# Turning a norm's blocks by transfers between SBUF tiles, and scaling two tiles at once, in a two-layer encoder trunk

## The chip, the core and the metric

The kernel runs on one core of a Trainium2 chip. The metric is the device time of one execution in microseconds (us). Five engines work beside each other and wait for one another by semaphores: TensorE (PE) multiplies matrices, VectorE (DVE), ScalarE (ACT) and GpSimd (POOL) work on elements, and SyncE (SP) issues transfers. A tile lies in SBUF with 128 partitions; matrix products are collected in PSUM.

## The reference, cut to what matters

A trunk of two layers on x of 256 rows by 2048 features, in float32. Layer 0 mixes by attention, layer 1 by a recurrent block (RG-LRU); each is followed by a gated feed-forward block (FFN). Each mixer and each FFN begins with an RMS norm.

```python
def rms_norm(x, g):
    xf = x.astype(jnp.float32)
    y = xf * lax.rsqrt(jnp.mean(xf * xf, axis=-1, keepdims=True) + EPS)
    return (y * g.astype(jnp.float32)).astype(x.dtype)

def swiglu(h, w_gate, w_up, w_down):
    return (jax.nn.silu(h @ w_gate) * (h @ w_up)) @ w_down
...
    for i in range(DEPTH):
        h = rms_norm(x, norm_mix[i])
        ...
        x = x + mix
        x = x + swiglu(rms_norm(x, norm_ffn[i]), ffn_w_gate[i], ffn_w_up[i], ffn_w_down[i])
    return x
```

## The kernel before

**Precision.** Each factor of a product is held as two parts, hi (a cast) and lo (the rest), and three products of parts make one product. A weight arrives in pieces of 512 KB (`raw`, issued on SP); ACT casts it (`hi`, L145 or L163) and DVE subtracts (`lo`, L146 or L164). Pieces stand in a ring of a few buffers: a load leaves once its buffer is free, and a cast waits till PE has read an older piece. Some column pairs of the FFN are multiplied with seven products in place of eight; their weight sums are L169 to L171 and their sums of x are the forms below.

**Norms.** x lies with rows in the partitions (`x_tm`); the products need it with features in the partitions. So each of the three norms inside the program (FFN of layer 0, mixer of layer 1, FFN of layer 1) has four turns, one for each group g of 512 features, begun as soon as the residual of that group is added (L347 or L349). One turn:

- the squares of x with their sums, on ACT (L444);
- DVE transposes 32x32 blocks of the group into `one` (L408), one instruction of 128x1024;
- 16 copies of 32x256 elements bring each block to its place in `two` (L416). ACT and POOL take eight each, in the last turn of a norm DVE eight, ACT four and POOL four;
- `scale`: four tiles `xg`, each with the gain of its features multiplied in, hi on ACT (L435) and lo on DVE (L436);
- in the FFN norms, for six of eight pairs of tiles, `form`: ACT scales the pair again (L466), POOL makes four sums (L472), ACT and DVE split them into `fh` and `fl` (L474, L475).

The row factor of a norm (`nr`, L480 to L505) is applied behind the products. For the recurrent layer `spread` puts it on a diagonal (`dg`, L492, DVE) and PE broadcasts it (L493).

**Order.** PE's order is written by hand; the order on the other engines comes from a scheduler that follows the order of the code and estimated times. An engine executes its own order strictly, so a waiting instruction holds up all behind it, on SP too. `one` and `two` have one buffer each: a next turn waits till the last one is read. The units of the FFN use the same names for their sums (L769 to L795) and call the same `turn_blocks`, with copies on ACT; this call stays.

Of the kernel before, what the change touches and what calls it, by code (L numbers as in the profile page):

```python
# [12 lines left out]
F32 = mybir.dt.float32  # L13
F32R = mybir.dt.float32r
AF = mybir.ActivationFunctionType
ALU = mybir.AluOpType
AX = mybir.AxisListType

P = 128
S = 256  # L20
D = 2048
KT = D // P
# [11 lines left out]
WIDE = 512  # L34
# [4 lines left out]
NW = D // WIDE  # L39
# [35 lines left out]
def trunk(ctx, tc, w, out):  # L75
    nc = tc.nc
    act, dve, pool, pe, sync = nc.scalar, nc.vector, nc.gpsimd, nc.tensor, nc.sync
# [3 lines left out]
    xp = ctx.enter_context(tc.tile_pool(name="xp", bufs=16))  # L81
# [7 lines left out]
    def nm(s):  # L89
        uid[0] += 1  # L90
        return f"{s}_{uid[0]}"

    def tmp(tag, shape=(P, S), dt=F32, bufs=2):
        pl = tp if tag in COMMON else scope[-1]
        return pl.tile(list(shape), dt, tag=tag, name=nm(tag), bufs=bufs)


    newest = {}
# [25 lines left out]
    def behind(key, i):  # L124
        if key in newest:
            follow(i, newest[key])
        newest[key] = i
        for rule in [rule for rule in ahead if key == rule[2]]:
            rule[0] -= 1
            if rule[0] == 0:  # L130
                follow(i, rule[1])
                ahead.remove(rule)
# [251 lines left out]
    x_tm = cst.tile([P, 2, D], F32, tag="x", name="x")  # L384
# [15 lines left out]
    def col(name, i):  # L400
        o = PK[name] + i
        return pk[:, o : o + 1]


    def turn_blocks(src, engines, own=None, spread=None):
        turned = tmp("one", (P, 2, WIDE), bufs=1)
        own = tmp("two", (P, 2, WIDE), bufs=1) if own is None else own
        dve.transpose(turned, src)  # L408
        t = own.rearrange("p a (b c) -> p (a b) c", c=S)

        def move(i):
            of = turned[32 * i : 32 * i + 32].rearrange("p a (k j c) -> p k a j c", k=4, j=4)
            for j in range(4):
                to = t[32 * j : 32 * j + 32].rearrange("p k (a i c) -> p k a i c", a=2, i=4)
                eng = engines[(4 * i + j) % len(engines)]
                m = (eng.copy if eng is act else eng.tensor_copy)(to[:, :, :, i, :], of[:, :, :, j, :])  # L416
                if spread is not None:
                    behind("cast", m)

        for i in range(4):  # L420
            move(i) if spread is None else spread.append(partial(move, i))
        return t

    class Norm:
        def __init__(self, gname, gofs):
            self.g = (gname, gofs)
            self.xs = []
            self.ss = tmp("ssq", (P, 2, NW))
            self.forms = {}

        def scale(self, src):
            k = len(self.xs)
            g = col(self.g[0], self.g[1] + k)
            t = xp.tile([P, 2 * S], F32R, tag="xg", name=nm("xg"), bufs=16)
            newest["xh"] = act.activation(t[:, :S], src, AF.Copy, scale=g)  # L435
            newest["xl"] = dve.scalar_tensor_tensor(  # L436
                t[:, S:], src, g, t[:, :S].bitcast(F32), ALU.mult, ALU.subtract
            )
            self.xs.append(t)
# [6 lines left out]
        def add(self, g):  # L446
            for a in range(2):
                self.square(g, a)
            if g == NW - 1:
                self.finish()  # L450
            self.turn(g, (act, pool) if g < NW - 1 else (dve, act, dve, pool))
            if g == NW - 1 and self.g[0] == "norm_mix":
                held.extend([[4, "cast", newest["xh"]], [4, "rest", newest["xl"]]])

        def turn(self, g, engines):
            t = turn_blocks(x_tm[:, :, g * WIDE : (g + 1) * WIDE], engines)
            for k in range(4):
                self.scale(t[:, k, :])
            for i in range(2):
                if self.g[0] == "norm_ffn" and 2 * g + i in SEVEN:  # L460
                    self.form(2 * g + i, t[:, 2 * i : 2 * i + 2, :])

        def form(self, c, src):
            v, t = (tmp("form", (P, 2 * S)).rearrange("p (a b) -> p a b", a=n) for n in (2, 4))
            for j in range(2):
                act.activation(v[:, j, :], src[:, j, :], AF.Copy, scale=col(self.g[0], self.g[1] + 2 * c + j))  # L466
            (a11, a21), (a12, a22) = ([v[:, j, a * P : (a + 1) * P] for a in range(2)] for j in range(2))
            for i, x, y, op in (
                (0, a21, a22, ALU.subtract), (1, a11, a21, ALU.subtract),
                (2, t[:, 0, :], a11, ALU.subtract), (3, a12, t[:, 2, :], ALU.add),  # L470
            ):
                pool.tensor_tensor(t[:, i, :], x, y, op)  # L472
            hi, lo = (tmp(f"f{n}", (P, 4, P), F32R, bufs=len(SEVEN)) for n in "hl")
            act.copy(hi, t)  # L474
            dve.tensor_tensor(lo, t, hi[:].bitcast(F32), ALU.subtract)  # L475
            self.forms[c] = [(hi[:, i, :], lo[:, i, :]) for i in range(4)]
# [160 lines left out]
    def attend(h, acc, dst):  # L637
# [23 lines left out]
        def scores():  # L661
# [18 lines left out]
            def turn():  # L680
# [15 lines left out]
                later(d_val, values)  # L696

            later(d_turn, turn)

        later(d_split, partial(split, qs, q))  # L700
# [342 lines left out]
```

## Time and profile before

| | |
|---|---|
| median of 3 runs | 1953.04 us (1952.99 to 1953.76) |
| the profiled execution, its own time | 1952.89 us |
| its span | 1951.1 us, at full granted clock (1.00) |
| layer 0, turns of the FFN norm | residual adds from 219.63 to 268.14 us, transposes from 224.83 to 270.13 |
| layer 1, turns of the mixer's norm | residual adds from 911.26 to 951.59 us |
| layer 1, turns of the FFN norm | residual adds from 1216.62 to 1265.26 us |

The profile gives busy times of each engine, the chain of work that ended last, groups of equal instructions, what each engine waited for, the busy time of chosen stretches ("x112" is the number of instructions in it), and a timeline of single instructions, where the brackets at the end hold the idle time before an instruction and what ended it. Times run from the start of the span. PE started a matmul of 512 columns each 0.227 us where nothing held it up; that makes about 112 in 25 us.

### The profile page before, as it was taken

What the parts mean: (1) busy time and instruction counts of PE and PEld (TensorE: products, weight loads), DVE (VectorE), ACT (ScalarE), POOL (GpSimd) and SP (SyncE); (2) the same over time, 40 slices, a digit from 0 to 9 for tenths busy, and PEclk for the clock granted to TensorE, in tenths of its full rate; (3) what the DMA queues carried; (4) which work ended last, traced back from release to release, by engine and by line L of the source; (5) the groups of instructions that cost most, each with busy time, mean ns of one, the idle gap of its engine ahead of it and who ended that gap; (6) DMA issues with size and microseconds to landing.
All of it is one profiled execution on the core that took longest, in us unless ns stands there. A gap on an engine that the chain in (4) does not pass through costs nothing.

```text
span 1951.1 us, 27630 instructions
## 1 busy us (share of the span) xinstructions
PE 1938.0 (99%) x9224; PEld 1624.0 (83%) x9224; DVE 1768.6 (91%) x2417; ACT 1448.3 (74%) x2358; POOL 401.3 (21%) x497
## 2 busy tenths in 40 slices
PE   9999999999999999999999999999999999999999
PEld 8898888788888888888899998887888888888887
DVE  7878698999999999998799997898999999999993
ACT  7677686777777777777698887866778776787772
POOL 0442250011101111010465450520101111011100
PEclk9999999999999999999999999999999999999999
DMA  8434746698878978787365556555878888788872
GB/s 328 156 127 152 248 158 197 196 272 236 248 233 243 262 240 246 235 244 246 126 223 188 189 164 245 175 194 174 253 236 248 245 248 253 231 246 251 246 257 86
DMA packets 131727, 426.42 MB, mean 219 GB/s; under 512 B 14720, under 2 KB 14976, under 8 KB 131584
## 3 DMA queue, kind: packets, MB, share of 16 engines
q1 hardware_dynamic: 108944, 383.21, 58.0%
q0 software_dynamic: 22496, 41.43, 11.9%
q8 instruction: 72, 1.18, 0.2%
q14 instruction: 71, 0.58, 0.1%
q10 hardware_dynamic: 144, 0.02, 0.0%
HBM read 382.13 MB, written 2.10 MB: 197 GB/s over the span
## 4 chain that ended last, share of the span: by engine, by line
PE 92%; DVE 4%; ACT 1%; issue 1%; DMA 1%; POOL 0%; SPq 0%; ACTq 0%; DVEq 0%; POOLq 0%
PE acc L326 14%; PE acc L323 14%; PE acc L324 14%; PE pm L326 11%; PE pm L323 11%; PE pm L324 11%; PE acc L294 8%; PE acc L292 4%; PE pm L306 1%; PE pm L307 1%; PE pm L305 1%; DVE lo L146 1%; ACT hi L145 1%; DVE lo L164 0%; DMA raw<-in_w_in_dram 0%
## 5 line engine op out<-in xcount | busy, mean ns | idle before, releaser
L146 DVE TENSOR_TENSOR lo<-raw,hi 128x1024 fp32r<-128x1024 f32 (+1 forms) x474 | 574.5, 1240 | 77.1 <-ACT hi L145 75.3
L145 ACT CAST hi<-raw 128x1024 fp32r<-128x1024 f32 (+1 forms) x474 | 478.4, 1045 | 116.5 <-PE acc L324 72.1
L326 PE MATMUL acc<-lo,xg 128*128 128x512 f32 x744 | 290.9, 391 | 2.0 <-DVE lo L146 1.8
L323 PE MATMUL acc<-hi,xg 128*128 128x512 f32 x744 | 290.0, 390 | 0.0
L324 PE MATMUL acc<-hi,xg 128*128 128x512 f32 x744 | 289.6, 389 | 0.0
L164 DVE TENSOR_TENSOR lo<-raw,hi 128x1024 fp32r<-128x1024 f32 x232 | 275.0, 1217 | 6.5 <-ACT hi L163 3.8
L294 PE MATMUL acc<-xg,hi 128*128 128x512 f32 x832 | 271.7, 397 | 0.6 <-ACT hi L145 0.6
L163 ACT CAST hi<-raw 128x1024 fp32r<-128x1024 f32 x232 | 234.6, 1048 | 41.0 <-issue 14.4
L176 POOL DMA_DIRECT2D raw<-raw x90 | 77.7, 863 | 903.9 <-DVE raw L174 369.5
L323 PE MATMUL pm<-hi,act 128*128 128x512 f32 x512 | 199.2, 389 | 0.0
L324 PE MATMUL pm<-hi,act 128*128 128x512 f32 x512 | 199.2, 389 | 0.0
L326 PE MATMUL pm<-lo,act 128*128 128x512 f32 x512 | 199.2, 389 | 0.0
L416 ACT COPY two<-one 32x256 f32<-32x256 f32 x420 | 169.7, 404 | 24.7 <-DVE one L408 16.5
L292 PEld LDWEIGHTS acc<-xg,lo 128*128 128x128 f32 x832 | 156.3, 188 | 35.4 <-DVE lo L146 2.8
L323 PE MATMUL acc<-hi,act 128*128 128x512 f32 x448 | 174.9, 390 | 0.4 <-DVE two L794 0.4
L326 PE MATMUL acc<-lo,act 128*128 128x512 f32 x448 | 174.4, 389 | 0.0
L324 PE MATMUL acc<-hi,act 128*128 128x512 f32 x448 | 174.4, 389 | 0.0
L292 PE MATMUL acc<-xg,lo 128*128 128x256 f32 x832 | 171.8, 281 | 1.2 <-DVE lo L146 1.2
L326 PEld LDWEIGHTS acc<-lo,xg 128*128 128x128 f32 x744 | 139.7, 188 | 34.1 <-DVE lo L146 5.4
L324 PEld LDWEIGHTS acc<-hi,xg 128*128 128x128 f32 x744 | 139.7, 188 | 29.2
L323 PEld LDWEIGHTS acc<-hi,xg 128*128 128x128 f32 x744 | 139.7, 188 | 28.6
L170 ACT CAST hi<-raw 128x512 fp32r<-128x512 f32 x232 | 137.1, 622 | 32.8 <-DVE raw L169 31.8
(221 smaller groups left out, 3852.1 us busy)
## 6 DMA issues: line engine op xcount, KB each, us to landing
raw<-in_w_gate_dram SPq DMA_DIRECT2D x176, 512.0 KB, 4.6
raw<-in_w_up_dram SPq DMA_DIRECT2D x176, 512.0 KB, 5.5
raw<-in_w_down_dram SPq DMA_DIRECT2D x176, 512.0 KB, 4.4
raw<-in_w_in_dram SPq DMA_DIRECT2D x64, 512.0 KB, 4.4
raw<-raw POOLq DMA_DIRECT2D x90, 256.0 KB, 5.8
raw<-in_w_q_dram SPq DMA_DIRECT2D x32, 512.0 KB, 3.8
raw<-in_w_o_dram SPq DMA_DIRECT2D x32, 512.0 KB, 4.2
x<-form POOLq DMA_DIRECT2D x64, 256.0 KB, 6.7
```

What stands on the lines that cost most here:

```text
L145: behind("cast", act.copy(hi[:, sl], raw[:, sl]))
L146: behind("rest", dve.tensor_tensor(lo[:, sl], raw[:, sl], hi[:, sl].bitcast(F32), ALU.subtract))
L163: behind("cast", act.copy(hi, src))
L164: behind("rest", dve.tensor_tensor(lo, src, hi[:].bitcast(F32), ALU.subtract))
L170: behind("cast", act.copy(hi, o))
L176: pool.dma_start(out=t1, in_=b11, accum_op=ALU.add)
L292: pe.matmul(acc[:, S:], w, xs[k][:, :S], start=False, stop=stop)
L294: pe.matmul(acc, w, xs[k], start=(k == 0), stop=stop)
L323: pe.matmul(o, xh, wh, start=start, stop=False)
L324: pe.matmul(o, xl, wh, start=False, stop=False)
L326: pe.matmul(o, xh, wl, start=False, stop=stop)
L416: m = (eng.copy if eng is act else eng.tensor_copy)(to[:, :, :, i, :], of[:, :, :, j, :])
```

## The change

`turn` calls a new `move_blocks`. It transposes in two instructions, in an order in which the 1 KB that one block row takes lies in one run, so that each of the 16 blocks is moved as 32 runs of 1 KB. In eleven of the twelve turns SP issues these 16 moves as transfers from `one` to `two`; the last turn of the mixer's norm still copies on DVE, ACT and POOL. `scaled` treats two tiles at once: ACT writes the scaled pair (`form`, two instructions of 128x256), ACT casts it in one instruction of 128x512, DVE subtracts in another; `form` takes the scaled pair from there, so that the second scaling (L466) goes. The tiles `xg` come as eight pairs in place of sixteen.

```diff
+    def move_blocks(src, engines):
+        turned = tmp("one", (P, 2, WIDE), bufs=1)
+        own = tmp("two", (P, 2, WIDE), bufs=1)
+        one, two = (t.rearrange("p a b -> p (a b)") for t in (turned, own))
+        for a in range(2):
+            dve.transpose(
+                one.rearrange("p (j a e) -> p j a e", j=4, a=2)[:, :, a, :],
+                src[:, a, :].rearrange("p (k j c) -> p j k c", k=4, j=4),
+            )
+        for i in range(4):
+            for j in range(4):
+                to, of = two[32 * j : 32 * j + 32, S * i : S * i + S], one[32 * i : 32 * i + 32, S * j : S * j + S]
+                if engines is None:
+                    sync.dma_start(out=to, in_=of)
+                else:
+                    eng = engines[(4 * i + j) % len(engines)]
+                    (eng.copy if eng is act else eng.tensor_copy)(to, of)
+        return two.rearrange("p (i a k c) -> p k a i c", i=4, a=2, k=4)
...
+        def scaled(self, src):
+            k = len(self.xs)
+            v = tmp("form", (P, 2 * S)).rearrange("p (a b) -> p a b", a=2)
+            for j in range(2):
+                to = v[:, j, :] if len(src.shape) == 3 else v[:, j, :].rearrange("p (a i c) -> p a i c", a=2, i=4)
+                act.activation(to, src[:, j], AF.Copy, scale=col(self.g[0], self.g[1] + k + j))
+            t = xp.tile([P, 2, 2 * S], F32R, tag="xg", name=nm("xg"), bufs=KT // 2)
+            hi, lo = t[:, :, :S], t[:, :, S:]
+            newest["xh"] = act.copy(hi, v)
+            newest["xl"] = dve.tensor_tensor(lo, v, hi.bitcast(F32), ALU.subtract)
+            self.xs += [t[:, j, :] for j in range(2)]
+            return v
...
-            self.turn(g, (act, pool) if g < NW - 1 else (dve, act, dve, pool))
+            self.turn(g, (dve, act, dve, pool) if g == NW - 1 and self.g[0] == "norm_mix" else None)
...
-            t = turn_blocks(x_tm[:, :, g * WIDE : (g + 1) * WIDE], engines)
-            for k in range(4):
-                self.scale(t[:, k, :])
+            t = move_blocks(x_tm[:, :, g * WIDE : (g + 1) * WIDE], engines)
             for i in range(2):
+                v = self.scaled(t[:, 2 * i : 2 * i + 2])
                 if self.g[0] == "norm_ffn" and 2 * g + i in SEVEN:
-                    self.form(2 * g + i, t[:, 2 * i : 2 * i + 2, :])
-
-        def form(self, c, src):
-            v, t = (tmp("form", (P, 2 * S)).rearrange("p (a b) -> p a b", a=n) for n in (2, 4))
-            for j in range(2):
-                act.activation(v[:, j, :], src[:, j, :], AF.Copy, scale=col(self.g[0], self.g[1] + 2 * c + j))
+                    self.form(2 * g + i, v)
+
+        def form(self, c, v):
+            t = tmp("form", (P, 2 * S)).rearrange("p (a b) -> p a b", a=4)
```

In the new code the transposes are L429, the transfers L437, the copies that stay L440, the scaling L455, its cast L458 and its subtraction L459; lines behind the change are higher by 31 (L492 is L523, L480 is L511).

The order on SP in the changed kernel, where the second and third turns of layer 0's FFN norm are inserted among the loads of FFN weights (before, these loads followed each other without the two rows of L437):

```order
L140 DMA raw_3283<-in_w_gate_dram 128x1024
L437 DMA two_2744<-one_2743 32x256 x16
L140 DMA raw_3301<-in_w_up_dram 128x1024
L140 DMA raw_3319<-in_w_gate_dram 128x1024
L140 DMA raw_3337<-in_w_up_dram 128x1024
L140 DMA raw_3355<-in_w_gate_dram 128x1024
L437 DMA two_2937<-one_2936 32x256 x16
L140 DMA raw_3373<-in_w_up_dram 128x1024
```

Each block of 16 transfers stands whole between two loads, and the load behind it waits for the sixteen issues.

The order on ACT in the changed kernel at the last turn of the same norm, up to the first instruction of unit 0's end (L800, L769 before); L163 and L145 are weight casts, L505 is the cast `fh`, which waits for POOL's sums:

```order
L163 CAST hi_3447<-raw_3439 128x1024
L455 ACTIVATE form_3168<-two_3149,pk 128x256 x2
L458 CAST xg_3171<-form_3168 128x2x256
L170 CAST ohi_3451<-raw_3439 128x512
L505 CAST fh_3179<-form_3174 128x512
L455 ACTIVATE form_3183<-two_3149,pk 128x256 x2
L170 CAST hi_3453<-raw_3438 128x512 x2
L145 CAST hi_3486<-raw_3485 128x1024
L145 CAST hi_3509<-raw_3508 128x1024
L458 CAST xg_3186<-form_3183 128x2x256
```

Before, all four scalings of this turn stood ahead of the weight casts of its last two pairs; now the last pair's cast stands behind `fh` and two weight casts.

The order on DVE at the turn that keeps its copies, the last one of the mixer's norm, before:

```order
L436 SCALAR_TENSOR_TENSOR xg_9201<-two_9183,pk,xg_9201 128x256
L436 SCALAR_TENSOR_TENSOR xg_9204<-two_9183,pk,xg_9204 128x256
L436 SCALAR_TENSOR_TENSOR xg_9207<-two_9183,pk,xg_9207 128x256
L436 SCALAR_TENSOR_TENSOR xg_9210<-two_9183,pk,xg_9210 128x256
L349 SCALAR_TENSOR_TENSOR x<-acc_9214,nr_3161,x 128x512
L408 STREAM_TRANSPOSE one_9339<-x 128x1024
L480 TENSOR_REDUCE nm_9329<-ssq_3211 128x2
L416 COPY two_9340<-one_9339 32x8x32 x2
L485 TENSOR_SCALAR nm_9329<-nm_9329 128x2
L416 COPY two_9340<-one_9339 32x8x32 x6
```

and now, from the copies to `dg`:

```order
L440 COPY two_9321<-one_9320 32x256 x8
L459 TENSOR_TENSOR xg_9185<-form_9182,xg_9185 128x2x256
L459 TENSOR_TENSOR xg_9191<-form_9188,xg_9191 128x2x256
L511 TENSOR_REDUCE nm_9310<-ssq_3189 128x2
L516 TENSOR_SCALAR nm_9310<-nm_9310 128x2
L459 TENSOR_TENSOR xg_9343<-form_9340,xg_9343 128x2x256
L534 TENSOR_TENSOR rsq_s_9314<-nm_9310,nr_9313 128x2
L459 TENSOR_TENSOR xg_9349<-form_9346,xg_9349 128x2x256
L535 SCALAR_TENSOR_TENSOR rsq_s_9314<-rsq_s_9314,nr_9313 128x2
L536 SCALAR_TENSOR_TENSOR nr_9313<-rsq_s_9314,nr_9313 128x2
L146 TENSOR_TENSOR lo_9515<-raw_9513,hi_9514 128x1024
L523 TENSOR_SCALAR dg_9438<-ident,nr_9313 128x128 x2
```

The subtractions of the turn before (here L459 for `xg_9185` and `xg_9191`) stood ahead of the second add as four L436 and now follow the copies; the mean (L511) comes behind them, and one weight split stands ahead of `dg`.

More of the change, by code (lines that the diff above doesn't have):

```diff
@@ L433, in scale @@
             g = col(self.g[0], self.g[1] + k)
-            t = xp.tile([P, 2 * S], F32R, tag="xg", name=nm("xg"), bufs=16)
+            if k % 2 == 0:
+                self.pair = xp.tile([P, 2, 2 * S], F32R, tag="xg", name=nm("xg"), bufs=KT // 2)
+            t = self.pair[:, k % 2, :]
             newest["xh"] = act.activation(t[:, :S], src, AF.Copy, scale=g)
```

## The prediction

> **What bounds the kernel now.** I read the page's busy shares and chain first, then the stretches in which TensorE (PE) falls short, then what it waits for there.
>
> ```profile
> span 1951.1 us, 27630 instructions
> ...
> PE 1938.0 (99%) x9224; PEld 1624.0 (83%) x9224; DVE 1768.6 (91%) x2417; ACT 1448.3 (74%) x2358; POOL 401.3 (21%) x497
> ...
> PE 92%; DVE 4%; ACT 1%; issue 1%; DMA 1%; POOL 0%; SPq 0%; ACTq 0%; DVEq 0%; POOLq 0%
> ```
>
> PE is busy for 1938.0 of 1951.1 us, so about 13 us are all that any edit off PE can win; the diff leaves PE's instructions as they are. The chain agrees: 92% of it is PE. The question is where those 13 us lie, and whether the norms' turns are among them. Three stretches of 25 us, with the busy time of each engine:
>
> ```profile
> 275.00:300.00 25.00, 25.00 (x112) 20.71 (x111) 24.87 (x41) 17.95 (x34) 10.83 (x15) 1.00 0.51 152
> 350.00:375.00 25.00, 22.84 (x97) 17.61 (x96) 24.23 (x29) 15.56 (x24) 1.71 (x2) 1.00 0.65 193
> 950.00:975.00 25.00, 23.90 (x138) 20.41 (x137) 24.25 (x47) 15.12 (x28) 12.58 (x24) 1.00 0.47 161
> ```
>
> The last turn of layer 0's FFN norm falls into the first stretch: PE is busy for all of it. The second lies behind unit 0 of the FFN, without any norm turn, and loses 2.16 us. The third holds the turn ahead of the recurrent layer and loses 1.10 us. PE's longest sums of waits:
>
> ```profile
> PE pm L323 <- ACT ohi L170: 2.4, 2, 1.2
> PE acc L326 <- DVE lo L146: 1.8, 3, 0.8
> ```
>
> Both are waits for weight splits in the units, not for a norm. DVE's timeline in layer 1 shows that this lateness does not come from the turns:
>
> ```profile
> 1298.33 0.69 DVE L770 TENSOR_TENSOR one<-one,pm 128x512 f32<-128x512 f32 x1 [1.33 <-PE pm L326]
> ...
> 1305.06 0.69 DVE L794 TENSOR_TENSOR two<-acc,two 128x512 f32<-128x512 f32 x1 [0.29 <-PE acc L326]
> 1305.67 5.76 DVE L146 TENSOR_TENSOR lo<-raw,hi 128x1024 fp32r<-128x1024 f32 x5
> ```
>
> DVE twice stands idle for PE's banks after the turns are over, 1.33 and 0.29 us. Whatever lead a cheaper turn gives it ends there; it then falls behind through its own work (five splits in a row, 5.76 us), in an order that the change leaves alone.
>
> **The change, part by part.** Copies and scalings go, by these rows of what writes or reads `two` (min/median/max ns), with one price for a cast of 128x512:
>
> ```profile
> L416 ACT COPY two<-one x420: 395/404/409, 226.6 to 1896.4; 32x256 f32<-32x256 f32 x140
> L416 POOL COPY two<-one x84: 387/396/1302, 226.4 to 1271.9; 32x256 f32<-32x256 f32 x84
> L435 ACT ACTIVATE xg<-two,pk x48: 492/495/512, 234.7 to 1275.6; 128x256 fp32r<-128x256 f32 x48
> L436 DVE SCALAR_TENSOR_TENSOR xg<-two,pk,xg x48: 438/476/686, 236.0 to 1279.3; 128x256 fp32r<-128x256 f32 x48
> ...
> L416 DVE COPY two<-one x40: 280/286/533, 279.2 to 1897.8; 32x256 f32<-32x256 f32 x40
> L466 ACT ACTIVATE form<-two,pk x24: 493/497/511, 236.3 to 1281.6; 128x256 f32<-128x256 f32 x24
> L771 DVE TENSOR_TENSOR two<-one,pm x22: 679/680/689, 302.9 to 1876.2; 128x512 f32<-128x512 f32 x22
> ```
>
> ```profile
> L474 ACT CAST fh<-form 128x512 fp32r<-128x512 f32 x6 | 3.7, 614 | 2.8 <-POOL form L472 2.8
> ```
>
> The twelve turns held 84 copies on ACT, 84 on POOL and 24 on DVE; the last mixer turn keeps 4, 4 and 8. So ACT sheds 80 x 0.404 = 32 us, POOL 80 x 0.396 = 32 us, DVE 16 x 0.286 = 5 us. Scaling on ACT was 72 x 0.495 = 36 us (L435, L466) and becomes 48 such steps plus 24 casts, 24 + 24 x 0.614 = 39 us. On DVE 48 x 0.476 = 23 us become 24 x 0.680 = 16 us. Transposes stay at about the same elements. All of this relief is worth nothing to the end: it falls where PE is at x112 already, and stops at the two waits for PE above.
>
> What is added is 176 transfers on SP and their landing. Nearest prices from the DMA view (KB, us to landing):
>
> ```profile
> raw<-in_w_gate_dram SPq DMA_DIRECT2D x176, 512.0 KB, 4.6
> ...
> out_dram<-x SPq DMA_DIRECT2D x8, 256.0 KB, 2.0
> ```
>
> I bound a block copy of 32 KB by 2.0 and 4.6 us from its issue and take 2.5, near the smaller row, because its bytes are an eighth of that one's. SP's rows around the last two turns of layer 0, which are the places where a block is inserted:
>
> ```profile
> 262.71 0.33 SPq L140 DMA_DIRECT2D raw<-in_w_up_dram  x1
> ...
> 278.11 0.33 SPq L140 DMA_DIRECT2D raw<-in_w_up_dram  x1
> 290.32 0.33 SPq L140 DMA_DIRECT2D raw<-in_w_gate_dram  x1
> ```
>
> An issue takes 0.33 us; with the semaphore wait between two of them I take 0.4, so a block holds SP for 6.4 us and has landed 9 us after its first issue. The third turn's block goes ahead of the load of 262.71, which then leaves near 268.5, some 5.8 us late, and lands 4.6 us later at 273.1. Its cast is this row of ACT:
>
> ```profile
> 273.84 1.06 ACT L145 CAST hi<-raw 128x1024 fp32r<-128x1024 f32 x1 [1.20 <-PE acc L324]
> ```
>
> It waits for a place in the ring that PE frees, so the load is still on time, and PE is several halves behind. The fourth block goes between 278.11 and 290.32, into 12 us in which SP did nothing: it delays no load and lands near 287.4. PE first wants the sixth form and the last pair of tiles here:
>
> ```profile
> 299.03 0.39 PE L323 MATMUL pm<-hi,fh 128*128 128x512 f32 x1
> ...
> 302.43 0.39 PE L323 MATMUL acc<-hi,xg 128*128 128x512 f32 x1
> ```
>
> From 287.4 I count on ACT: two scalings and a cast, 1.6 us; POOL's four sums, 3.6 us; fh and fl, 1.3 us: the form is ready near 294, 5 us early. Behind it ACT does two scalings, two casts of 128x512 and two of 128x1024 before the last pair's cast, about 5 us: near 299, 3 us early. With the upper bound for each landing the eight transfers that may be on their way at once add 2.1 us to the ninth's issue and 2.1 to the end: 4.2 us later, so the form still comes by 298 and the last pair by about 303, half a microsecond late. Term: 0, at most 1 us a layer.
>
> **The turn that stays on the engines** is the one beside which PE has no cover. DVE and ACT before:
>
> ```profile
> 951.59 0.74 DVE L349 SCALAR_TENSOR_TENSOR x<-acc,nr,x 128x512 f32<-128x512 f32 x1
> 952.36 1.25 DVE L408 STREAM_TRANSPOSE one<-x 128x1024 f32<-128x1024 f32 x1
> ...
> 954.69 2.16 DVE L416 COPY two<-one 32x256 f32<-32x256 f32 x6
> ...
> 957.48 1.69 DVE L436 SCALAR_TENSOR_TENSOR xg<-two,pk,xg 128x256 fp32r<-128x256 f32 x4
> 959.20 0.48 DVE L492 TENSOR_SCALAR dg<-ident,nr 128x128 f32<-128x128 f32 x2
> ```
>
> ```profile
> 956.94 1.71 ACT L435 ACTIVATE xg<-two,pk 128x256 fp32r<-128x256 f32 x4 [1.13 <-DVE two L416]
> ```
>
> After, the second add no longer stands behind four L436 and starts about 1.6 us sooner, near 950.0; both transposes are done by 952.0, the eight copies (0.36 each) by 954.9. The earlier pairs' two subtractions now follow, to 956.1. ACT makes its four copies and two squares to 955.3, then, at 0.43 a scaling, four of these, two small steps of the root and two casts, to about 958.4. The second subtraction follows that cast, to 959.1, then two small steps and, new in this place, one weight split of 1.2 us ahead of L492. So dg starts near 960.5 to 960.8 where it started at 959.20: 1.3 to 1.6 later. PE there:
>
> ```profile
> 958.68 0.40 PE L294 MATMUL acc<-xg,hi 128*128 128x512 f32 x1
> 959.80 0.68 PE L493 MATMUL pm<-dg,ones 128*128 128x128 f32 x4 [0.73 <-DVE dg L492]
> ```
>
> ```profile
> 974.34 0.50 PE L292 MATMUL acc<-xg,lo 128*128 128x256 f32 x2 [0.37 <-DVE lo L146]
> ```
>
> L493 moves by the same 1.3 to 1.6. At 974.34 PE waits again, 0.37 us, for a split whose load left long before; a later PE waits there that much less. Net 0.9 to 1.2; bounds 0 (the contiguous copies run at DVE's smallest 0.28) and 2.5 (nothing absorbed, tiles late too).
>
> The Trainium skill has a rule on these copies ("VectorE: DVE Perf Modes", What auto-detection actually checks): one source and destination in SBUF with even outer dimensions already run two elements a cycle. By it the new shape gains nothing over the old one. No row of before has the new shape, so the trace cannot decide it. By the rule the sum below stays as it is; if the old shape was the slower one, it would be about 0.9 lower.
>
> **Sum:** 1952.89 (the profiled execution's own time) + 0 for the block transfers + 0.9 = 1953.8. That execution is 0.15 under the median of 1953.04, so no correction is made.
>
> **Rivals.** *Late blocks, slower.* If a small transfer's landing takes 7 us, the ninth issue of the fourth block waits until 285.9, the last leaves by 288.7 and lands at 295.7: 8.3 us later than I count, 3.3 to 5.3 more than the margins of 5 and 3. Two layers lose that much each, with the middle 1960 to 1964; it decides from about 5 us a landing. For it: the DMA row of 4.6 and the fact that weight loads fill the same queue just ahead. Against it: the margins, and loads whose readers wait for PE. Chance 0.16.
>
> The Trainium skill ("DMA: Bandwidth & Descriptors", Rules for kernel authors) says of many small transfers that under 64 KB one pays mostly overhead, and its section on queues that a completion signal lands behind earlier writes of the same DMA engine. Both speak for this rival; no transfer of this size between SBUF tiles is in the trace of before.
>
> *Relief reaches the units, faster.* If the lead on DVE and ACT outlives the waits at L770 and L794, the loss of the 350 stretch and its twin could halve: 2 x 2.16 / 2 = 2.2, with the splits behind them perhaps 4: 1949.8. Against it: the DVE rows of layer 1. Chance 0.10.
>
> *Nothing happens.* The copies are not what the end waits for, and the middle turn gains by its earlier transposes what it loses in order: 1952.9. Chance 0.20. My forecast, 1952.5 to 1955.5, has 0.48; the rest, 0.06, is a middle turn that costs over 2.5 us.
>
> **Numbers.** 0.2% is 3.9 us, about what a measurement of this kernel can tell from no change. Slower by more: 0.16 and a third of the last case, 0.18. Faster by more: some of the relief case, 0.06. Same: the rest, 0.76. The range goes from 1950.3, inside the relief case, to 1958.5, which leaves most of the late blocks out.
>
> **What would show it.** Right: x112 in the stretches from 225 to 300 as before; small transfers landing in 2 to 3 us; the wait of L493 for dg grown from 0.73 to about 2; the two unit stalls unchanged to a few hundredths. Wrong: PE waits for a norm's tiles or forms near 299 to 303, or at their like in layer 1; ACT idle for `two` by more than a few microseconds; load landings late ahead of L145; or less than 2 us lost at 350.

## The result and the profile after

The changed kernel took **1964.34 us** (median of 4 runs, 1963.08 to 1966.01) where the kernel before took 1953.01 us (4 runs, 1952.15 to 1953.76): a ratio of **1.0059, 95% interval 1.0041 to 1.0076**. It is slower, by 11.3 us, and lies 5.8 us above the upper end of the predicted range. The profiled execution took 1963.08 us, its span is 1961.3 us.

From the page after: span, busy shares, the chain by engine, and its shares by line.

```profile
span 1961.3 us, 27668 instructions
...
PE 1940.9 (99%) x9224; PEld 1624.8 (83%) x9224; DVE 1756.8 (90%) x2389; ACT 1420.6 (72%) x2278; POOL 354.2 (18%) x417
...
PE 87%; DVE 5%; ACT 3%; issue 2%; DMA 2%; SPq 1%; POOL 0%; ACTq 0%; DVEq 0%; POOLq 0%
PE acc L326 13%; PE acc L323 13%; PE acc L324 13%; PE pm L324 11%; PE pm L326 11%; PE pm L323 11%; PE acc L294 8%; PE acc L292 4%; DVE lo L146 2%; PE pm L306 1%; PE pm L307 1%; PE pm L305 1%; SPq L437 1%; ACT hi L145 1%; ACT two L416 1%
```

The relief came: DVE 11.8 us less and ACT 27.7, as the prediction's prices give (about 12 and 29), POOL 47.1 where they give 32. None of it shows in the time. Instead SP's queue, at 0% of the chain before, now holds 1% of it by the line of the new transfers (L437).

Where the 10.2 us of span went can be read by laying the two traces side by side: the same matmul, found by its place in PE's order (which the change leaves alone), starts so much later than before. At the times of the trace of before, in us:

| trace of before at | 200 | 290 | 304 | 320 | 346 | 900 | 957 | 960 | 975 | 1310 | 1365 | 1946 |
|---|---|---|---|---|---|---|---|---|---|---|---|---|
| after, later by | -0.27 | -0.27 | 1.84 | 2.31 | 2.89 | 2.79 | 9.62 | 10.47 | 10.03 | 10.15 | 10.43 | 10.23 |

Two places hold nearly all: **3.2 us between 290 and 346** (the end of layer 0's FFN norm) and **7.7 us around 957** (the norm ahead of the recurrent layer), of which 0.44 comes back at once. Layer 1's FFN norm costs 0.3. The same three stretches as before, with the busy time of PE, PEld, DVE, ACT and POOL, the granted clock, the DMA share and GB/s:

```profile
275.00:300.00 25.00, 24.24 (x107) 19.59 (x105) 19.39 (x29) 16.52 (x31) 9.80 (x13) 1.00 0.73 260
350.00:375.00 25.00, 22.81 (x97) 17.57 (x96) 24.20 (x30) 14.67 (x23) 1.22 (x2) 1.00 0.60 203
950.00:975.00 25.00, 18.86 (x94) 15.85 (x93) 16.72 (x32) 14.73 (x32) 5.44 (x13) 0.86 0.40 132
```

The first stretch was full (x112) and now is not (x107). The second, the stalls in the unit, is as it was (x97). The third has lost 44 matmuls, and its clock is at 0.86. What PE waited for (total, times, longest):

```profile
PE acc L294 <- DVE xg L459: 5.1, 1, 5.1
...
PE pm L324 <- DVE fl L506: 1.0, 1, 1.0
```

The largest wait is now a single one of 5.1 us for a norm's tile, and `fl` of a form is new in this list. Both are behind transfers. First the transfers themselves, from the view of line L437: min/median/max ns of one issue, and us from issue to landing.

```profile
L437 SPq DMA_DIRECT2D two<-one x176: 507/588/1772, 225.9 to 1294.8; - x176
...
DMA to landing us min/median/max: 1.7/1.9/8.2
```

The median landing is quick, 1.9 us, but 53 of the 176 took more than 2.5 us, one of them 8.2. The issue is slow everywhere: 0.588 us in the median, where the loads on which the prediction was built took 0.33. SP's queue, at the fourth block of layer 0, the three blocks ahead of the recurrent layer, and the fourth block of layer 1:

```profile
280.05 13.53 SPq L437 DMA_DIRECT2D two<-one  x16
...
917.90 11.21 SPq L437 DMA_DIRECT2D two<-one  x16
...
932.28 10.84 SPq L437 DMA_DIRECT2D two<-one  x16
...
946.24 10.29 SPq L437 DMA_DIRECT2D two<-one  x16
...
1283.04 12.31 SPq L437 DMA_DIRECT2D two<-one  x16
```

A block holds SP for 10 to 13.5 us; the prediction had 6.4. Where nothing else holds SP, one issue starts 0.63 us after the other, and 16 of them take 10.1. What the longer blocks have on top can be read from the start and the landing of each transfer. In all twelve traces of this case no more than eight transfers of SP and ACT together are under way at a time. Ahead of the fourth block of layer 0 stand nine loads of 512 KB that SP, held up by the third block, sent in 7 us (272.73 to 279.63); before, they left one by one from 262.71 to 278.11. They landed 4.4 to 9.1 us after their issue. The fourth to eighth transfers of the block start at 282.46, 283.74, 285.01, 286.29 and 288.01, each within 0.02 us of the landing of the load eight places ahead (282.45, 283.73, 285.00, 286.28, 287.99), and the first seven take 8.2 down to 3.5 us to land, against 1.9 for the last nine. So this block has 10.1 us of issues and 3.4 us of waits for loads to land; in the middle a block has 1.1, 0.7 and 0.2 us over the 10.1.

Now PE, with the two late places of layer 0 and those of the recurrent layer:

```profile
298.86 0.39 PE L323 MATMUL pm<-hi,fh 128*128 128x512 f32 x1
300.27 0.50 PE L324 MATMUL pm<-hi,fl 128*128 128x512 f32 x1 [1.03 <-DVE fl L506]
...
304.36 0.50 PE L324 MATMUL acc<-hi,xg 128*128 128x512 f32 x1 [0.39 <-DVE xg L459]
...
957.99 0.40 PE L294 MATMUL acc<-xg,hi 128*128 128x512 f32 x1
963.53 0.79 PE L294 MATMUL acc<-xg,hi 128*128 128x512 f32 x1 [5.14 <-DVE xg L459]
...
970.27 0.68 PE L524 MATMUL pm<-dg,ones 128*128 128x128 f32 x4 [1.00 <-ACT hi L145]
```

Behind the two waits of layer 0 stands SP's block: ACT at the fourth block of layer 0, then DVE at the third turn and at the last turn of the middle.

```profile
294.98 0.91 ACT L455 ACTIVATE form<-two,pk 128x256 f32<-128x256 f32 x2 [3.86 <-DMA two<-one]
```

```profile
944.53 1.31 DVE L429 STREAM_TRANSPOSE one<-x 128x512 f32<-128x512 f32 x2 [5.29 <-DMA two<-one]
...
958.19 1.31 DVE L429 STREAM_TRANSPOSE one<-x 128x512 f32<-128x512 f32 x2 [4.29 <-DMA two<-one]
959.85 2.90 DVE L440 COPY two<-one 32x256 f32<-32x256 f32 x8 [0.36 <-ACT form L455]
962.78 1.29 DVE L459 TENSOR_TENSOR xg<-form,xg 128x512 fp32r<-128x512 f32 x2
```

In layer 0 the last issue ends at 293.58 (280.05 + 13.53), ACT starts at 294.98 after 3.86 us of waiting for that landing, and the form reaches PE 1.03 us late. In the middle DVE waits 5.29 us till the second block has landed before it may transpose the third turn, so that the third block starts only at 946.24. The third block's last issue ends at 956.53 (946.24 + 10.29). Only when it has landed may the last turn transpose into `one`, at 958.19, after DVE has stood still for 4.29 us. Copies, scaling and subtraction follow, and PE gets its tile at 963.53.

Around this pause PE's granted clock falls. Stretches of 3 us, columns as above:

```profile
961.00:964.00 3.00, 0.47 (x1) 0.47 (x2) 2.91 (x7) 1.98 (x5) 0.67 (x2) 0.51 0.56 216
964.00:967.00 3.00, 3.00 (x11) 2.52 (x11) 0.40 (x3) 3.00 (x11) 0.00 (x0) 0.50 0.00 0
967.00:970.00 3.00, 2.27 (x11) 1.69 (x10) 2.89 (x8) 3.00 (x6) 0.95 (x6) 0.85 0.00 0
```

It is at 0.50 by the end of the pause and for about 4 us after it. So the 7.7 us of the middle are 5.3 of waiting (957.99 to 963.53, less the 0.23 of one matmul), some 2.1 of half clock, and 0.3 at L524 (1.00 where it was 0.73).

The Trainium skill ("TensorE: Matmul & The Clock Gate", Part 1) says that TensorE falls to half rate after an idle window of about 3.4 us and comes back after about 3.4 us of busy time. The rows of 0.50 and some 4 us here agree. Shorter pauses, of about 2 us, were followed by a lower clock in two runs too (last section); there the measurement decides.

### The profile page after: what moved, and what is told of

Its sections match the earlier page's. It is cut to its first block, busy times and chain, and to the rows that moved or that the text cites. A ratio compares the mean times of both kernels' runs of the same rounds, so it can differ in the third digit from the quotient of the medians.

```text
span 1961.3 us, 27668 instructions
## 1 busy us (share of the span) xinstructions
PE 1940.9 (99%) x9224; PEld 1624.8 (83%) x9224; DVE 1756.8 (90%) x2389; ACT 1420.6 (72%) x2278; POOL 354.2 (18%) x417
## 3 DMA queue, kind: packets, MB, share of 16 engines
q0 software_dynamic: 22496, 41.43, 11.8%
## 4 chain that ended last, share of the span: by engine, by line
PE 87%; DVE 5%; ACT 3%; issue 2%; DMA 2%; SPq 1%; POOL 0%; ACTq 0%; DVEq 0%; POOLq 0%
PE acc L326 13%; PE acc L323 13%; PE acc L324 13%; PE pm L324 11%; PE pm L326 11%; PE pm L323 11%; PE acc L294 8%; PE acc L292 4%; DVE lo L146 2%; PE pm L306 1%; PE pm L307 1%; PE pm L305 1%; SPq L437 1%; ACT hi L145 1%; ACT two L416 1%
## 5 line engine op out<-in xcount | busy, mean ns | idle before, releaser
L145 ACT CAST hi<-raw 128x1024 fp32r<-128x1024 f32 (+1 forms) x474 | 478.8, 1046 | 126.3 <-PE acc L324 80.4
L163 ACT CAST hi<-raw 128x1024 fp32r<-128x1024 f32 x232 | 235.1, 1049 | 46.0 <-issue 14.1
L169 DVE TENSOR_TENSOR raw<-raw,raw 128x512 f32<-128x512 f32 x232 | 150.7, 690 | 3.2
```

What stands on the lines that cost most here:

```text
L145: behind("cast", act.copy(hi[:, sl], raw[:, sl]))
L163: behind("cast", act.copy(hi, src))
L169: behind("rest", dve.tensor_tensor(o, x, y, op))
```

## The experiments

Edits are against the changed kernel. The first four runs test where the loss sits and whose it is: **S**, the issue on SP's queue and the chain of blocks through the one buffer; **L**, the landing, and transfers and loads in each other's way. From the second set on, **P** stands beside them: the pairs, that is, scaling and casting two tiles at once in the turn beside which PE has no cover. Each ratio is against the kernel before on the same chip, with its 95% interval. "Later" numbers are worked out like the table above: layer 0 from 290 to 346, the middle from 945 to 962, in us of the trace of before. An edit also changes the order that the scheduler gives the other engines, so small terms can move with it.

### No transfers at all

```diff
-            self.turn(g, (dve, act, dve, pool) if g == NW - 1 and self.g[0] == "norm_mix" else None)
+            self.turn(g, (dve, act, dve, pool) if g == NW - 1 else (act, pool))
```

> All twelve turns copy on the engines (ACT and POOL, the last turn of a norm DVE, ACT and POOL); the two transposes in the new order, the contiguous copies and the scaling of two tiles at once stay. Theory S (SP takes 0.6 us for each of these transfers, so a block holds SP for 10 us, and blocks in a row hold each other up through the one buffer of `one`): no transfers, no loss beside dg's new place, 1952.5 to 1954.5, and PE's wait of 5.1 us for xg in the middle turn is gone. Rival C (the loss comes from the new order and the paired scaling): 1960 or more, the waits for xg and fl stay. Rival L (the small transfers get in the way of the weight loads on the DMA engines): as S, 1953.

Measured: 1956.94 against 1952.53, 1.0022 (1.0012 to 1.0031). Three fifths of the loss are gone with the transfers, but 4.4 us stay, more than S gave: 1.1 in layer 0 and 3.1 in the middle. ACT, DVE and PE at the last turn of the middle:

```profile
958.05 1.71 ACT L455 ACTIVATE form<-two,pk 128x256 f32<-128x256 f32 x4 [1.19 <-DVE two L440]
959.66 1.12 ACT L458 CAST xg<-form 128x512 fp32r<-128x512 f32 x2
```

```profile
955.78 2.17 DVE L440 COPY two<-one 32x256 f32<-32x256 f32 x6
...
960.29 1.29 DVE L459 TENSOR_TENSOR xg<-form,xg 128x512 fp32r<-128x512 f32 x2 [1.76 <-ACT xg L458]
```

```profile
961.04 0.50 PE L294 MATMUL acc<-xg,hi 128*128 128x512 f32 x1 [1.61 <-DVE xg L459]
...
962.54 0.68 PE L524 MATMUL pm<-dg,ones 128*128 128x128 f32 x4 [0.54 <-DVE dg L523]
```

ACT scales all four tiles (1.71 us) before it casts the first pair, and DVE waits 1.76 us for that cast. So there is a second cost, without any transfer: P. The 1.1 us of layer 0 are in the units' waits for weight splits, at 308.24 (0.63 us from matmul to matmul) and 342.91 (0.76), beside an ACT whose order at the norm's end is the changed one. Of the 3.1 us in the middle some 1.4 are PE at a lower clock behind the wait (0.58 from 964 to 967). The six copies of contiguous blocks took 2.17 us, the six in the old shape 2.16, so the new shape gains nothing, as the prediction's sum had it.

### Transfers in the FFN norms only, and in the mixer's norm only

```diff
-            self.turn(g, (dve, act, dve, pool) if g == NW - 1 and self.g[0] == "norm_mix" else None)
+            self.turn(g, None if self.g[0] == "norm_ffn" else (dve, act, dve, pool) if g == NW - 1 else (act, pool))
```

> Transfers only in the two FFN norms; the mixer's norm copies on the engines in all four turns. Theory S: the middle loses its 7.6 us, layer 0 keeps its 3: 1955 to 1957, with the first PE wait near 299 as in the changed kernel. Rival C: 1960 or more, the middle keeps its wait. Rival L: as S in the middle, and the loads behind the blocks in layer 0 land late.

Measured: 1960.12, 1.0037 (1.0023 to 1.0052); more than S gave. The middle is later by only 1.35, with the same wait of 1.61 us for `xg` as without transfers but at full clock. Layer 0 is later by 5.3: its fourth block takes SP even longer than in the changed kernel, and ACT gets it later.

```profile
280.42 15.17 SPq L437 DMA_DIRECT2D two<-one  x16
```

```profile
296.99 0.91 ACT L455 ACTIVATE form<-two,pk 128x256 f32<-128x256 f32 x2 [3.94 <-DMA two<-one]
```

Of these 15.17 us, 5.1 are over the 10.1 of sixteen issues. The load just ahead of the block took 10.0 us to land, the block's first transfer 9.8. That is a sign of L, beside S, at this block.

The other way round:

```diff
+            self.turn(g, None if g < NW - 1 and self.g[0] == "norm_mix" else (dve, act, dve, pool) if g == NW - 1 else (act, pool))
```

> Transfers only in the first three turns of the mixer's norm; the two FFN norms copy on the engines. Theory S: layer 0's 3 us are gone, the middle's 7.6 stay: 1960 to 1961.5, with PE's wait for xg of about 5 us. If the middle's loss depends on delays inherited from the FFN norm of layer 0, it would be smaller: 1957.

Measured: 1962.08, 1.0048 (1.0033 to 1.0063), half a microsecond over the expected range. Layer 0 is later by 1.1, as without any transfer; the middle by 8.45, with one wait of 5.9 us for L459. Each set of transfers costs in its own place, by its own mechanism, and the middle's is the larger.

### The transfers on two queues

```diff
-                    sync.dma_start(out=to, in_=of)
+                    (sync, act)[j % 2].dma_start(out=to, in_=of)
```

> As the changed kernel, but every second transfer of a block is issued by ACT in place of SP; number, size and bytes of the transfers are the same. Theory S: each block takes SP 5 us instead of 10, the three blocks of the mixer's norm end 10 us or more earlier, PE's wait of 5.1 us for xg goes; ACT pays some 5 us a turn, of which it was idle for 7: 1953 to 1957. Rival L: the same transfers meet the same loads, the waits stay: 1961 to 1965.

Measured: **1972.72, 1.0107 (1.0090 to 1.0124)**, worse than either theory gave. Some blocks did get short; SP's half of one of them, then ACT and PE:

```profile
248.86 5.16 SPq L437 DMA_DIRECT2D two<-one  x8
```

```profile
225.81 7.17 ACTq L437 DMA_DIRECT2D two<-one  x8
...
271.46 1.14 ACT L170 CAST hi<-raw 128x512 fp32r<-128x512 f32 x2 [3.25 <-DMA two<-one]
```

```profile
272.13 0.79 PE L323 MATMUL pm<-hi,fh 128*128 128x512 f32 x1 [2.52 <-ACT hi L170]
```

Eight issues on each engine, side by side, at the same price as one engine's (0.589 us median on SP, 0.602 on ACT). What S left out is that ACT is a worker: while it issues it does nothing else, and behind that its casts of weights come late, so PE waits in places that were covered. Layer 0 is later by 9.2 (counted from 200, since some 6 of them come ahead of 290), the middle by 4.2, layer 1 by 5.4 more. In the middle PE's wait for `xg` fell from 5.1 to 1.9 us, as S has it, but the time as a whole decides nothing between S and L.

### Half of the block on POOL

```diff
-                if engines is None:
+                if engines is None and j % 2:
+                    pool.tensor_copy(to, of)
+                elif engines is None:
                     sync.dma_start(out=to, in_=of)
```

> As the changed kernel, but of each block of 16 moves POOL copies eight and SP issues eight transfers. Theory S (SP's 0.63 us for each issue, in a row through one buffer): a block holds SP for 5 us, the three blocks of the mixer's norm end 15 us earlier, PE's wait of 5.1 us there falls to e1's 1.6, and layer 0's two waits near 299 and 304 go: 1956 to 1958.5. Rival L (transfers and loads on the same DMA engines): half the transfers keep about half of the loss over e1: 1960 or more.

Measured: **1954.04 against 1952.81, 1.0006 (0.9996 to 1.0016)**, less than S gave and no difference that can be told from none. POOL has time to spare (21% busy in this run), and the eight issues hold SP for 5 to 6.3 us, in the later two blocks of the middle for under 5. One of these:

```profile
925.53 4.95 SPq L439 DMA_DIRECT2D two<-one  x8
```

```profile
PE acc L294 <- DVE xg L461: 1.3, 1, 1.3
```

Layer 0 is later by nothing (-0.08 at 352). With half the transfers to issue, PE's waits behind them are gone in both places. This run halves the issues and the transfers under way together, so it does not tell S from L in layer 0. What is left is a wait of 1.3 us for `xg`, P's.

### Shorter transfers

```diff
-                    sync.dma_start(out=to, in_=of)
+                    for r in range(0, 32, 16):
+                        sync.dma_start(out=to[r : r + 16], in_=of[r : r + 16])
```

> Each transfer of 32 runs of 1 KB is split into two of 16 runs, 32 to a block; bytes and runs are the same. If SP's time goes by the run, an issue takes 0.3 us and the time stays at 1963 to 1966. If it goes by the transfer, an issue stays at 0.59 us, a block holds SP for 20 us, and the three blocks of the mixer's norm alone add some 30 us: 1990 to 2030.

One run. Its time, 2831.7 us, can't be compared, since the granted clock was 0.651 in it (0.64 to 0.68 in every stretch); SP's issue times are still of use:

```profile
L438 SPq DMA_DIRECT2D two<-one x352: 507/587/1318, 308.0 to 1887.7; - x176
```

An issue of 16 runs takes what one of 32 runs takes, 0.587 and 0.588 us. **The price goes by the transfer, not by its runs or bytes**, as far as these two sizes tell.

### One block of the middle alone

As the half on POOL, but the first two turns of the mixer's norm copy on ACT and POOL, and the third sends all 16 moves to SP:

```diff
+            last = g == NW - 1
+            third = (sync,) if g == 2 else (act, pool)
+            self.turn(g, ((dve, act, dve, pool) if last else third) if self.g[0] == "norm_mix" else None)
```

> As e7, but in the mixer's norm only the third turn's block goes by transfers, all sixteen on SP; the first, second and last turns copy on the engines. Theory S in its full form (three blocks in a row, each waiting through the one buffer of `one` and `two` for the one before): a single block of 10 us can start at its own transposes near 938, ends near 950 and holds nothing up: PE's wait for xg 1 to 2 us as in e1 and e7, 1954 to 1956. If one block of 10 us ahead of the last turn is enough, whatever stands before it: a wait for xg of 4 us or more, 1958 or more.

Measured: 1955.08, 1.0009 (1.0000 to 1.0019). SP's block, and DVE's transposes of the last turn:

```profile
937.87 10.74 SPq L437 DMA_DIRECT2D two<-one  x16
```

```profile
950.27 1.31 DVE L429 STREAM_TRANSPOSE one<-x 128x512 f32<-128x512 f32 x2
```

The block is as long as in the changed kernel (10.74 against 10.29), but starts 8.4 us earlier (3.4 of them are PE's smaller lateness in this run, 5.0 the shorter wait for the buffer), and the transposes wait for nothing. So it isn't one slow block that holds the last turn; it is **three in a row, each of which can only begin when the one before has left the buffer**. A second buffer for `one` and `two` was not tried.

### The pairs: by tile, with the old copies, and undone

Three runs on P. Without transfers, but with each tile scaled into hi, scaled again, and subtracted by itself:

```diff
+            for j in range(2):
+                hi, lo = t[:, j, :S], t[:, j, S:]
+                g = col(self.g[0], self.g[1] + k + j)
+                for to in (hi, v[:, j, :]):
...
+                    newest["xh"] = act.activation(o, src[:, j], AF.Copy, scale=g)
+                newest["xl"] = dve.tensor_tensor(lo, v[:, j, :], hi.bitcast(F32), ALU.subtract)
```

> All turns copy on the engines as in e1, but each tile is made at once: ACT scales it into hi and again into the float32 form, DVE subtracts, tile by tile, so that no tile waits for the scalings and the cast of a pair. Theory P (what e1 lost in the middle is the pair: four scalings ahead of the first cast, one pass more before the first tile): PE's wait of 1.6 us for xg in the middle goes or falls below 0.5, 1953 to 1955. Rival B (e1's loss comes from the transposes in two pieces and the contiguous copies): 1956 to 1958, the wait stays.

Measured: 1955.86 against 1952.81, 1.0017 (1.0008 to 1.0026), 0.9 us above P's range. The wait for `xg` is gone and another stands in its place: eight scalings on ACT where there were four hold up DVE's subtractions, and with them `dg`.

```profile
PE pm L525 <- DVE dg L524: 1.6, 1, 1.6
```

Without transfers, with pairs, but with the copies and the transposes of before:

```diff
-            t = move_blocks(x_tm[:, :, g * WIDE : (g + 1) * WIDE], engines)
+            t = turn_blocks(x_tm[:, :, g * WIDE : (g + 1) * WIDE], engines)
```

> The block copies of the kernel before (one transpose, copies in the old shape) with the scaling of two tiles at once. Theory P: as e1, 1956 to 1958, with a wait for xg of 1.5 to 2 us in the middle. Rival B: as before, 1952 to 1954.

Measured: 1958.73, 1.0029 (1.0018 to 1.0041), over P's range too. In the middle the wait is the one that P gives:

```profile
PE acc L294 <- DVE xg L459: 1.6, 1, 1.6
```

The middle is later by 1.3. The 2.8 in layer 0 (1.1 without the old copies) and 3.1 between 352 and 945, with two waits of PE at 851.95 and 890.90 for work of the units (1.13 and 1.15 us), are in no theory's expectation and stay unexplained; the profiled execution, at 1960.59, also lies 1.9 us over the median.

Last, the half on POOL with the one turn of the middle as it was before the change, copies, scaling and all:

```diff
+            if engines is not None:
+                t = turn_blocks(src, engines)
+                for k in range(4):
+                    self.scale(t[:, k, :])
+                return
```

> As e7 (eight of sixteen moves by SP, eight by POOL, in eleven turns), but the last turn of the mixer's norm wholly as in the kernel before: one transpose, copies in the old shape, each tile scaled straight from `two` on ACT and DVE. Theory P says that e7's last microsecond is the pair's longer way to the first tile in that turn: the wait for xg (1.3 us) goes, dg comes as before, 1952.3 to 1953.4, no difference to before. If e7's rest came from the transfers, it stays at 1954 with a wait for xg over 1 us. Faster than before by more than 1 us is expected by neither.

Measured: **1952.64 against 1952.94, 0.9998 (0.9989 to 1.0007)**: no difference. DVE's copies and subtractions, then PE:

```profile
954.10 2.16 DVE L416 COPY two<-one 32x256 f32<-32x256 f32 x6
...
956.91 1.69 DVE L472 SCALAR_TENSOR_TENSOR xg<-two,pk,xg 128x256 fp32r<-128x256 f32 x4
```

```profile
959.23 0.68 PE L532 MATMUL pm<-dg,ones 128*128 128x128 f32 x4 [0.32 <-DVE dg L531]
```

The wait for `xg` is gone, and `dg` comes 0.32 us late where it was 0.73 late before. This version still has ACT 26 us less busy than before (1422.3 for 1448.3), and gains nothing by it. No version that ran beats the kernel before.

## Why the prediction was wrong, point by point

The sum had 0 for the block transfers, at most 1 us a layer, and 0.9 for the turn on the engines, at most 2.5. Measured were 3.2 and 0.3 us in the two layers, and 7.7.

**What bounds the kernel: right.** PE does, and relief on DVE, ACT and POOL was worth nothing. With half of the transfers, and the pairs of all turns but one, kept, the time is 0.9998 of before.

**The issue: wrong, and this is the step that failed.** "An issue takes 0.33 us; with the semaphore wait between two of them I take 0.4, so a block holds SP for 6.4 us." The row was that of a lone load of 512 KB between DRAM and SBUF. The issue between two SBUF tiles took 0.588, with 0.63 from one to the next: 16 x 0.63 = 10.1. The prediction bounded the landing from both sides and the issue not at all, although no row of before had such a transfer. With half the issues on SP, PE has no wait behind transfers left, in layer 0 or in the middle, and DVE's waits for them ahead of the transposes fall from 17.6 us to 0.6.

**The landing: right in the median, wrong where it counted.** Taken as 2.5 us, measured 1.9. The Trainium skill ("DMA: Bandwidth & Descriptors", Anatomy of one DMA, SWDGE (gpsimd) path) gives a fixed cost of about 2.0 us for a transfer issued from GpSimd. These are issued from SP, and their median of 1.9 is close to it. But in the block that PE waits for, the fourth of layer 0, the first transfers took up to 8.2, behind loads that the third block had held up and that then left bunched. The prediction moved one such load by 5.8 us and gave it 4.6 to land; it did not count that the loads behind it leave together and hold the eight places.

**What the two cost in layer 0.** The fourth block lands at 294.87 where 287.4 stood, 7.5 us later: 1.6 by its later start, 3.7 by slower issues, 3.4 by waits for loads, less 1.2 for a shorter landing behind the last issue. The margins of 5 and 3 us were well read (PE waits at exactly these two places, for the sixth form and the last pair) and are used up: 1.3 and 0.7 us lost there. Without the 3.4 the block would land near 291.5, an estimate from these numbers; PE's two waits are 1.0 and 0.4 us long. So the slow issues of this block alone need not have cost layer 0 these waits. The bunched loads come from the third block, which the slow issue had lengthened as well. No run parts the two. The other 1.1 of layer 0 are two waits for weight splits at 310.50 (0.56 us from matmul to matmul) and 345.17 (0.75). They are in the kernel without transfers too (0.63 and 0.76), so they need no transfer; but they are not in the kernel with half on POOL, which has the same pairs. The new orders on ACT and DVE, which the prediction showed and then gave no price, are the likely cause; it is not shown. Layer 1's fourth block costs next to nothing: ACT's first scaling behind it starts 9.5 us before PE first wants the sixth form (1296.66 and 1306.17), in layer 0 only 3.9 us before (294.98 and 298.86).

**The turn that stays on the engines: incomplete, and the larger part of the loss.** The prediction worked out its own instructions and the 1.3 to 1.6 us by which `dg` moves, and bounded the whole at 2.5. It left out that the three turns ahead of it go through the same single `one`, on SP, one after another: three times a block and its landing against three times the copies of before. DVE was in fact ready for the transposes at 953.9 (958.19 - 4.29). In times of before (2.8 earlier) that is 951.1, sooner than the 952.36 there, as the step said. But it then waited 4.29 us for the third block. "Tiles late too" was in the bound, yet at 2.5 and with another cause. The runs put the whole at 7.7, of which 1.0 to 3.1 stay without a chain of three full blocks.

**That rest was misread too.** The step counted the late `dg` (0.9 to 1.2 net) and not that a pair's first tile is ready only when both are scaled and cast. This gives a wait for `xg` of 1.3 to 1.7 us in five kernels with pairs (without transfers 1.61, with transfers in the FFN norms only 1.61, with the old copies 1.55, with half on POOL 1.28, with one block alone 1.66), and none where that turn was restored. `dg` itself hides behind that wait: PE waits 0.54 us or less for it in these five, where it waited 0.73 before. Where the clock stayed at 1.00 the middle lost 1.0 to 2.1 us; only without transfers came a stretch of lower clock on top, and 3.1. The prediction had no term for the clock anywhere.

**Absorption: right.** 0.44 us came back behind the middle (10.47 to 10.03), forecast 0.37. **The unit stalls: right.** In layer 0 they are 1.23 and 1.57 us from matmul to matmul in both traces, to the hundredth, in layer 1 within 0.03.

**Two small sums.** The prediction says that the total would be about 0.9 lower if the old copies were the slower ones; eight copies at 0.28 in place of 0.36 us are 0.6. It changes nothing, since they were not. And POOL's relief was priced with a median of 0.396 us a copy; the mean of its copies before is 0.536. That too changes nothing in the time.

**The rivals.** "Late blocks" (1960 to 1964, chance 0.16) came within half a microsecond of the time, but in part by luck. It named the loads that fill the queue just ahead, and for the fourth block of layer 0 long landings do lengthen the block: it lands at 294.87 where the rival said 295.7, though the waits are for the loads ahead and not for the block's own first transfer. It was wrong that this costs 3.3 to 5.3 us in each layer: the blocks cost 2.0 in layer 0 and nothing that can be seen in layer 1. And it had nothing for the chain in the middle, where sixteen issues make 10.1 of the 10.3 to 11.2 us of a block. Issue time was no rival. The Trainium skill ("DMA: Bandwidth & Descriptors", Issuing engines are not separate DMA queues) says that issuing from several engines saves only the sequencer's time to initiate a DMA, which is usually small beside the DMA itself. Here one issue of 0.63 us is a third of a landing of 1.9, and sixteen are five times it.

## What to carry to other kernels

Many small transfers in place of copies move work to the issuing queue: multiply their number by a measured issue time of the same kind of transfer, and where no row has that kind, bound it as widely as the landing. Then ask which loads the block holds up: they leave bunched, and the next block waits behind them. Where tiles have one buffer, count the whole chain of turns through it, up to the one that nothing covers, and not that one's instructions alone. And merging two tiles' steps saves instructions but makes the first tile as late as the second: beside a PE that has no other work, this costs more than it saves.

## What the runs showed of the hardware that was not expected

- An issue of an SBUF-to-SBUF transfer took 0.588 us on SP, for 32 runs of 1 KB and for 16 alike, against 0.33 for a lone load of 512 KB and 0.38 for loads sent back to back. SP and ACT issued side by side at 0.589 and 0.602, so the cost is the engine's own, and on ACT it displaces other work.
- In all twelve traces no more than eight transfers of SP and ACT together were under way at a time. With eight loads of 512 KB under way, the next issues came 1.2 to 1.7 us apart, one for each load that landed, where 0.63 was the pace without them.
- A pause of PE of 5.54 us from matmul to matmul was followed by some 4 us at a granted clock of 0.50. With pauses of 2.01 and 0.93 us (no transfers) the clock fell to 0.58 from 964 to 967, and with one of 2.14 us (by tile) to 0.66 from 961 to 964. With 2.01 and 0.57 us (transfers in the FFN norms only) and 2.06 and 0.58 us (one block alone) it stayed at 1.00. What decides at this length stays open.
- One run had a granted clock of 0.651, about the same in every stretch. What it comes from stays open.
